# Seven down products in another order, splits between convolution steps and a rearranged last norm: a hybrid encoder block on one Trainium2 core

## The chip, the cores and the metric

The kernel runs on one core of one Trainium2 chip. The metric is the device time of one execution in microseconds (us). An execution has one TensorE (PE, matmuls; its weight loads are listed as PEld), VectorE (DVE), ScalarE (ACT), GpSimd (POOL) and a queue of transfers that SyncE issues (SP). Every engine works through its own list of instructions in order and waits where an operand, a buffer or a bank of PSUM is not ready. The kernel before took 1299.77 us (median of three runs, 1299.09 to 1300.25).

## The reference

A sequence of 1024 frames plus 16 meta tokens, 1024 wide, passes one layer: a mixer (retention heads and forgetting-attention heads), then a gated feed-forward part with a causal convolution, then a last RMS norm. All arithmetic is float32. The change touches the feed-forward part and the last norm only:

```
up = einsum('bld,df->blf', h, w_up)          # 1024 -> 2 x 2816
a, b = split(up, 2)
acc = conv_b + sum_j a_pad[:, j:j+L] * conv_w[j]     # 3 taps
h = h + einsum('blf,fd->bld', silu(acc) * b, w_down) # 2816 -> 1024
out = h * rsqrt(mean(h*h) + eps) * final_norm_g      # per frame
```

## The kernel before, in words

Everything is kept transposed: features lie on the 128 partitions, frames along the free axis. The result is eight tiles `H[0..7]` of 128 features x 1024 frames (`H0` is the first half of the frames, columns 0 to 511, `H1` the second).

**Up stage.** The 2816 hidden features are 22 tiles (`ft`). For each, the up projection is done as seven half-size products in place of eight (Strassen's scheme in Winograd's form, `SEQ`); then `conv1` and `conv2` do the convolution, SiLU and the gate, `u`, and `tsum` makes the differences T1 to T4 that the down stage needs of it. `u` and the T tiles are stored to HBM (`uB..`, `uT..`). `sd_sum` makes the sums S1 to S4 of the down weights and stores those (`wS..`).

**Down stage.** Again seven products of 512-wide halves (`DSEQ`): each is a sum over 11 k-tiles (`KH`), and each k-tile has a weight tile and an activation tile, loaded from HBM into `d_raw` and split into a high and a low fp32r part by `d_unit` (ACT casts the high part, `split_u`, L1197; DVE subtracts for the low part, L1198). A k-tile is then 4 blocks `j` x 3 matmuls (high x high, high x low, low x high), `d_mm`, L1384. With `g` counting k-tiles over all products, the main loop over `g` issues the matmuls of `g` and then splits ahead, up to k-tile `g + 4`. Split units live in a ring: six for the first six k-tiles (shared with the up stage), then twelve. Banks `X` (psa, psc) collect products 0, 2, 4, 6, banks `Y` (psb, psx) products 1, 3, 5; products 0, 1 and 4 start a fresh sum. `d_post` adds a finished sum to `H`.

The seven products run as 0, 1, 2, 3, 4, 5, 6. Product 0 reads the plain weights `A11` and `uB11`; product 1 reads `S2` and `T2`, whose last tile comes from the last `ft`. Product 5 finishes the lower four `H` tiles in `H0`, product 4 their `H1`, product 2 the upper four in `H0`, and product 6 the upper four in `H1`.

**Last norm.** Frames are taken in three chunks, `FCH`: chunk 0 is `H0` (512 frames), chunks 1 and 2 are the halves of `H1` (256 each). `sq_add` squares on ACT and adds on POOL (chunk 0) or DVE; `f_norm` sums over partitions with a matmul by ones (`nps`), takes the root, makes diagonal matrices (`dg`) and spreads the factor with a matmul (`pr`); `f_emit` multiplies, on ACT and POOL or on DVE by the bit masks `OUTE`, and SP stores. In product 6 the last three k-tiles (`NL = 3`) are held back and done as two halves of 256 frames, block by block, so that `H1` can be added, squared and summed block by block.

PE, DVE, ACT and POOL follow the written program order (`tc.manual_schedule`); the order of SP's transfers is chosen by the framework's scheduler.

Of the kernel before, what the change touches and what calls it, by code (L numbers as in the profile page):

```python
# [81 lines left out]
def tile_hymba_block(ctx, tc, xt, xn, wrv0, wrv1, wft, wout, wup, wdn, small, cst, rope, dtab, out):  # L82
# [1181 lines left out]

    cas, us = {}, {}

    def conv1(ft):
# [3 lines left out]
        act.activation(ca, at[:, 0:NF], AF.Copy, scale=cw[0])  # L1271
        dve.scalar_tensor_tensor(ca, at[:, 1:1 + NF], cw[1], ca, op0=ALU.mult, op1=ALU.add)
# [104 lines left out]
    X = Y = None  # L1377

    def d_mm(g, j, c, n, new):
        i, kt = divmod(g, KH)  # L1380
        a_, b_ = d_units[g, 0], d_units[g, 1]
        ps = (X, Y)[i in (1, 3, 5)][j]
        for m, (wi, hl) in enumerate(((0, 0), (0, 1), (1, 0))):
            pe.matmul(ps[:, c:c + n], lhsT=a_[:, wi, j * P:(j + 1) * P], rhs=b_[:, hl, c:c + n],  # L1384
                      start=(new and m == 0), stop=(kt == KH - 1 and m == 2), skip_group_check=i in (2, 3, 5, 6))
# [3 lines left out]
    with tc.manual_schedule(engines=ENG):  # L1389
# [256 lines left out]
        for g in range(6, 8):  # L1646
# [25 lines left out]
        def sq_add(ci, d):  # L1672
            c0, n = FCH[ci]
            hsl = H[d][:, c0:c0 + n]
            if ci not in acs:
                acs[ci] = es.tile([P, n], F32, name=f"ac{ci}")
                act.activation(acs[ci], hsl, AF.Square)
            else:
                sq = es.tile([P, 512], F32, tag="sq4", name="sq4", bufs=4)[:, :n]
                act.activation(sq, hsl, AF.Square)  # L1680
                (pool if ci == 0 else dve).tensor_tensor(acs[ci], acs[ci], sq, op=ALU.add)  # L1681

        prd = {}

        def f_norm(ci):
            c0, n = FCH[ci]
            m = n // P
            ps = (pb, px)[ci % 2].tile([P, 512], F32, tag=("psb", "psx")[ci % 2], name="nps")
            for j in range(m):
                pe.matmul(ps[:, j:j + 1], lhsT=acs[ci][:, j * P:(j + 1) * P], rhs=ones, start=True, stop=True)  # L1690
# [1 line left out]
            act.activation(r, ps[:, :m], AF.Sqrt, bias=epsc, scale=1.0 / 1024)
            dve.reciprocal(r, r)
            pr = (pb, px)[ci % 2].tile([P, 512], F32, tag=("psb", "psx")[ci % 2], name="pr")[:, :n]
            for j in range(m):
                dg = es.tile([P, P], F32, tag="dg", name="dg", bufs=4)
                dve.tensor_scalar(dg, idf, r[:, j:j + 1], None, op0=ALU.mult)  # L1697
                pe.matmul(pr[:, j * P:(j + 1) * P], lhsT=on, rhs=dg, start=True, stop=True)  # L1698
            prd[ci] = [pr, None]
            if OUTE[ci]:  # L1700
                prd[ci][1] = es.tile([P, n], F32, name=f"prs{ci}")
                act.copy(prd[ci][1], pr)

        fo = {}

        def f_emit(ci, d):
            c0, n = FCH[ci]
            pr, prs = prd[ci]
            m = 512 // n
            if d % m == 0:  # L1710
                fo[ci] = es.tile([P, m, n], F32, tag="fo", name="fo", bufs=8)
            ot = fo[ci][:, d % m, :]
            hsl = H[d][:, c0:c0 + n]
            g = sm[:, S_LG + d:S_LG + d + 1]
            if OUTE[ci] & (1 << d):
                act.activation(ot, hsl, AF.Copy, scale=g)  # L1716
                pool.tensor_tensor(ot, ot, prs, op=ALU.mult)
            else:
                dve.scalar_tensor_tensor(ot, hsl, g, pr, op0=ALU.mult, op1=ALU.mult)  # L1719
            if d % m == m - 1:  # L1720
                sp.dma_start(out[(d + 1 - m) * P:(d + 1) * P, c0:c0 + n].rearrange("(a p) n -> p a n", p=P), fo[ci])

        NL = 3
        for g in range(7 * KH):
            i, kt = divmod(g, KH)
# [14 lines left out]
            if i == 5 and 2 <= kt < 10:  # L1740
                if kt < 6:
                    sq_add(0, kt - 2)
                elif kt < 10:
                    sq_add(1, kt - 2)
                    sq_add(2, kt - 2)
            if i == 6:
                if kt in (1, 2):
                    sq_add(0, 2 + 2 * kt)
                    sq_add(0, 3 + 2 * kt)
                if kt == 3:  # L1750
                    f_norm(0)
                if 4 <= kt < 8:
                    f_emit(0, 2 * kt - 8)
                    f_emit(0, 2 * kt - 7)
            for _ in range(3):
                if d_next[0] < 2 * (g + 5):
                    d_unit()
        for hf in range(2):
            for j in range(4):
                for g in range(7 * KH - NL, 7 * KH):  # L1760
                    d_mm(g, j, 256 * hf, 256, False)
                hsl = H[j][:, 512 + 256 * hf:768 + 256 * hf]
                dve.tensor_tensor(hsl, X[j][:, 256 * hf:256 * hf + 256], hsl, op=ALU.add)  # L1763
# [84 lines left out]
```

## Time and profile before

| | |
|---|---|
| median of three runs | 1299.77 us |
| profiled execution: its own time, its span | 1297.7 us, 1295.6 us |
| PE / PEld busy, share of the span | 97% / 92% |
| DVE, ACT, POOL busy | 71%, 45%, 28% |
| transfers: mean busy share, whole span | 46.6% |
| down stage, first matmul to last output | from 1056.96 us to the end |

The profiled execution's span is 2.1 us under its own time. Times within it are given from the start of the span. The views used below: the table of busy time and granted clock in chosen stretches; the list of waits, which names for each engine whom it waited for; and the instructions in order of time, where one row may stand for several equal neighbours (x6) and the bracket gives the idle time ahead and what ended it. In the rows, L1384 is the matmul line of `d_mm`, L1197 and L1198 the two halves of a split, L1690 and L1698 the two small matmuls of the norm, L1763 the last addition into `H1`.

### The profile page before, as it was taken

The numbers are of one execution on the slowest core, as the hardware profiler recorded it, in microseconds if no ns is written. First come the engines' busy times: TensorE is split into PE (matmuls) and PEld (weight loads), VectorE is DVE, ScalarE is ACT, GpSimd is POOL, SyncE is SP. The second block draws the span as 40 slices with busy tenths as digits, with TensorE's granted clock in tenths as the row PEclk, the third lists the DMA queues.
The fourth block names the chain that finished last, engine by engine and source line by source line (L and its number), as shares of the span: only waits on it lengthen the run. The fifth ranks groups of instructions, "written<-read, shape, count | busy, mean of one in ns | idle before, by whom it ended". The sixth has DMA issues, their size and how long they took to land. (4 is left out here: it accounts for less than half of the span.)

```text
span 1295.6 us, 24143 instructions
## 1 busy us (share of the span) xinstructions
PE 1253.1 (97%) x9243; PEld 1187.8 (92%) x9243; DVE 916.6 (71%) x1571; ACT 589.4 (45%) x1171; POOL 365.2 (28%) x301
## 2 busy tenths in 40 slices
PE   8999999999999989989899999999999989999995
PEld 8999999999999989989899999999999988888884
DVE  5776546556565666658978778788898976855565
ACT  7773442456445553545533334334343335444552
POOL 0154244000000000022166456465464632300132
PEclk9999999999999999999999999999999999999998
DMA  8533124114223535364255354355655679666633
GB/s 284 178 95 97 36 68 128 38 44 124 52 62 95 156 109 166 102 206 131 69 193 163 118 167 143 127 180 176 222 183 184 212 263 348 233 195 192 190 104 117
DMA packets 110947, 192.76 MB, mean 149 GB/s; under 512 B 15143, under 2 KB 50295, under 8 KB 110832
## 3 DMA queue, kind: packets, MB, share of 16 engines
q1 hardware_dynamic: 110832, 191.23, 46.6%
q8 instruction: 72, 1.18, 0.4%
q14 instruction: 43, 0.35, 0.1%
HBM read 132.59 MB, written 52.21 MB: 143 GB/s over the span
## 5 line engine op out<-in xcount | busy, mean ns | idle before, releaser
L1198 DVE TENSOR_TENSOR d_u<-d_raw,d_u 128x512 fp32r<-128x512 f32 x154 | 118.0, 820 | 60.7 <-ACT d_u L1197 60.6
L1197 ACT CAST d_u<-d_raw 128x512 fp32r<-128x512 f32 x154 | 87.1, 619 | 95.1 <-PE psx L1384 44.3
L666 PE MATMUL psD<-xl,f_hi 128*128 128x256 f32 (+2 forms) x448 | 129.3, 289 | 0.0
L666 PE MATMUL psD<-xh,f_hi 128*128 128x256 f32 (+2 forms) x448 | 128.1, 286 | 0.4 <-DVE fq L672 0.4
L666 PE MATMUL psD<-xh,f_lo 128*128 128x256 f32 (+2 forms) x448 | 128.2, 286 | 0.0
L1193 POOL TENSOR_TENSOR S<-u_raw 128x512 f32<-128x512 f32 x42 | 59.0, 1406 | 202.9 <-DVE unit L1211 168.9
L1232 PE MATMUL psb<-B0T,unit 128*128 128x256 f32 x780 | 104.0, 282 | 1.0 <-DVE unit L1211 0.9
L1232 PE MATMUL psb<-B1T,unit 128*128 128x256 f32 x780 | 103.4, 281 | 0.7 <-ACT B1T L1158 0.6
L797 ACT ACTIVATE pf<-psS 128x272 f32<-128x272 f32 (+4 forms) x112 | 49.7, 451 | 114.0 <-PE psS L787 67.3
L1232 PEld LDWEIGHTS psb<-B0T,unit 128*128 128x128 f32 x780 | 97.2, 189 | 1.7 <-DVE unit L1211 1.4
L1232 PEld LDWEIGHTS psb<-B1T,unit 128*128 128x128 f32 x780 | 97.1, 189 | 1.1 <-ACT B1T L1158 0.8
L666 PEld LDWEIGHTS psD<-xh,f_hi 128*128 128x128 f32 x448 | 84.7, 189 | 0.9 <-DVE fq L672 0.6
L666 PEld LDWEIGHTS psD<-xl,f_hi 128*128 128x128 f32 x448 | 84.4, 188 | 0.4
L666 PEld LDWEIGHTS psD<-xh,f_lo 128*128 128x128 f32 x448 | 84.5, 189 | 0.1
L1390 POOL MEMSET on<- 128x128 f32 x1 | 0.2, 205 | 297.0 <-PE psS L791 297.0
L1211 DVE TENSOR_TENSOR unit<-S,unit 128x512 fp32r<-128x512 f32 x87 | 78.7, 906 | 2.6 <-ACT unit L1207 2.3
L733 DVE TENSOR_REDUCE mx<-psS 128x1 f32<-128x512 f32 (+6 forms) x120 | 59.0, 539 | 29.8 <-PE psS L730 20.9
L183 PE MATMUL psj<-rv_hi,xh 128*128 128x256 f32 (+1 forms) x264 | 76.3, 293 | 2.6 <-DVE z L287 2.2
L1207 ACT CAST unit<-S 128x512 fp32r<-128x512 f32 x87 | 54.1, 622 | 53.3 <-POOL S L1193 52.6
L1271 ACT ACTIVATE ca<-at,sm 128x1024 f32<-128x1024 f32 x22 | 25.3, 1152 | 112.5 <-DVE at L1263 112.5
L184 PE MATMUL psj<-rv_lo,xh 128*128 128x256 f32 (+1 forms) x264 | 75.5, 288 | 0.2 <-DVE rv_lo L118 0.2
L185 PE MATMUL psj<-rv_hi,xl 128*128 128x256 f32 (+1 forms) x264 | 75.3, 288 | 0.0
(347 smaller groups left out, 3581.8 us busy)
## 6 DMA issues: line engine op xcount, KB each, us to landing
u_raw<-wup SPq DMA_DIRECT2D x44, 512.0 KB
sd<-wdn SPq DMA_DIRECT2D x88, 128.0 KB
uB<-u SPq DMA_DIRECT2D x44, 256.0 KB
wS<-sd SPq DMA_DIRECT2D x88, 128.0 KB
d_raw<-wS SPq DMA_DIRECT2D x44, 256.0 KB
d_raw<-uT SPq DMA_DIRECT2D x44, 256.0 KB
d_raw<-wdn SPq DMA_DIRECT2D x33, 256.0 KB
d_raw<-uB SPq DMA_DIRECT2D x33, 256.0 KB
```

The lines of the kernel that those rows point to most:

```text
L183: pe.matmul(ps[:, :w], lhsT=x_h, rhs=w_h[:, c0:c0 + w], start=(k == 0), stop=False)
L184: pe.matmul(ps[:, :w], lhsT=x_h, rhs=w_l[:, c0:c0 + w], start=False, stop=False)
L185: pe.matmul(ps[:, :w], lhsT=x_l, rhs=w_h[:, c0:c0 + w], start=False, stop=(k == KT - 1))
L666: pe.matmul(ps[:, :n], lhsT=w_, rhs=X(e, k, t0 + a, n), start=(k == 0 and i == 0), stop=(k == KT - 1 and i == 2))
L733: dve.tensor_reduce(mxs[s][:R - q_, j, ci:ci + 1], ps[:R - q_, :n], axis=mybir.AxisListType.X, op=ALU.max)
L797: act.activation(pf[:r, a:b], ps[:r, a:b], AF.Exp)
L1193: (eng or pool).tensor_tensor(t, s_[x], s_[y], op=o)
L1197: act.copy(t[:, 0], src)
L1198: eng.tensor_tensor(t[:, 1], src, f(t[:, 0]), op=ALU.subtract)
L1207: act.copy(t[:, 0], srcs[ft][nm])
L1211: dve.tensor_tensor(t[:, 1], srcs[ft][SEQ[i][0]], f(t[:, 0]), op=ALU.subtract)
L1232: pe.matmul(ps[:, :n], lhsT=w[:, wi, k * P:(k + 1) * P], rhs=o[:, hl, k, :], start=(new and j == 0), stop=(j == 11), skip_group_check=not new)
```

## The change

- **Order of the products.** `DORD = (1, 0, 3, 2, 5, 4, 6)`: banks now alternate Y, X, Y, X, Y, X, X. Product 4 and product 6 are neighbours in the same banks, so each block's sum of product 4 is added to `H` (`d_post(4, j)`) ahead of that block's first matmul of product 6.
- **Splits in the last convolution.** Six more `d_unit` calls stand between the steps of the last `ft`: one ahead of `post(.., 6, 1)`, one inside `conv1`, two ahead of `conv2`, two behind it. Five k-tiles are thus split, or given out to be, before the down loop starts, where it was two.
- **Unit ring in two pools.** The ring of twelve is now eight buffers (`du`) and four (`du2`), used in the same turn.
- **Chunk 0 of the norm is earlier.** Products 5 and 2 are done after the fifth place, so squares are taken in places five and six, and `nps`, root, `dg` and `pr` of chunk 0 stand in the sixth place (its k-tiles 6, 8 and 9). Its eight outputs are emitted in the last product, one per k-tile, all on DVE.
- **Last product.** `NL` goes from 3 to 5. `f_norm` is cut in four (`f_nps`, `f_dg`, `f_bc`, `f_prs`) that stand apart, with matmuls of the next block between them. The last squares are not added on DVE but summed by more `nps` matmuls (`last`). `dg` is made on ACT but for one. The lower four outputs of chunk 1 and three of chunk 2 are pre-scaled on ACT (`f_pre`) and finished on POOL. The last two outputs of chunk 2 are stored one by one.

```
@@ the last ft @@
         d_unit()
         post(NFT - 1, 6, 0)
+        d_unit()
         post(NFT - 1, 6, 1)
-        conv1(NFT - 1)
+        conv1(NFT - 1, d_unit)
+        for _ in range(2):
+            d_unit()
         conv2(NFT - 1)
+        for _ in range(2):
+            d_unit()
         for _ in tsum(NFT - 1):
             pass
...
+    DORD = (1, 0, 3, 2, 5, 4, 6)
...
-            i, kt = divmod(g, KH)
+            i, kt = DORD[g // KH], g % KH
...
-        pl, nb = (Wu, 6) if g < 6 else (dp[1], 12)
+        lo = (d_next[0] - 13) % 12 < 8
+        pl, nb = (Wu, 6) if g < 6 else (dp[1], 8) if lo else (dp[2], 4)
...
-                (pool if ci == 0 else dve).tensor_tensor(acs[ci], acs[ci], sq, op=ALU.add)
+                if ci and d > (2, 2, 1)[ci] and d < 4:
+                    last[ci].append(sq)
+                else:
+                    (pool if ci == 0 and d < 4 else dve).tensor_tensor(acs[ci], acs[ci], sq, op=ALU.add)
...
+            src = [acs[ci]] + last.get(ci, [])
             for j in range(m):
-                pe.matmul(ps[:, j:j + 1], lhsT=acs[ci][:, j * P:(j + 1) * P], rhs=ones, start=True, stop=True)
+                for x, a_ in enumerate(src):
+                    pe.matmul(ps[:, j:j + 1], lhsT=a_[:, j * P:(j + 1) * P], rhs=ones,
+                              start=(x == 0), stop=(x == len(src) - 1))
...
-        NL = 3
+        NL = 5
         for g in range(7 * KH):
-            i, kt = divmod(g, KH)
-            if i < 6 or kt < KH - NL:
+            pos, kt = divmod(g, KH)
+            if pos < 6 or kt < KH - NL:
                 for j in range(4):
-                    d_mm(g, j, 0, 512, i in (0, 1, 4) and kt == 0)
-            if i and kt == 0:
+                    if pos == 6 and kt == 0:
+                        d_post(4, j)
+                    d_mm(g, j, 0, 512, DORD[pos] in (0, 1, 4) and kt == 0)
+            if 0 < pos < 6 and kt == 0:
                 for j in range(4):
-                    d_post(i - 1, j)
+                    d_post(DORD[pos - 1], j)
...
+            if pos == 5:
+                if 1 <= kt < 5:
+                    sq_add(0, 3 + kt)
+                if kt == 6:
+                    f_nps(0)
+                if kt == 8:
+                    f_dg(0)
+                if kt == 9:
+                    f_bc(0)
+            if pos == 6:
+                if kt < 4:
+                    sq_add(1, 4 + kt)
+                    sq_add(2, 4 + kt)
+                if kt < KT:
+                    f_emit(0, kt)
...
+                if hf and j == 0:
+                    f_nps(1)
+                    f_dg(1)
+                if hf and j == 1:
+                    f_bc(1)
+                    f_prs(1)
+                    for d in range(4, KT):
+                        f_emit(1, d, True)
                 sq_add(1 + hf, j)
-                if hf and j == 1:
-                    f_norm(1)
-        for d in range(KT):
+                if hf and j < 3:
+                    f_pre(2, 4 + j)
+        f_nps(2)
+        for d in range(3):
             f_emit(1, d)
-        f_norm(2)
-        for d in range(KT):
+        f_dg(2)
+        f_emit(1, 3)
+        f_bc(2)
+        f_prs(2)
+        for d in (4, 5, 6):
+            f_emit(2, d, True)
+        for d in (0, 1, 2, 3, 7):
             f_emit(2, d)
```

Three places show how instructions move. First DVE at the end of the last `ft` (`at`, `ca`, `u`, `T2o` are the last convolution's steps, `d_u` are low halves of splits), of before:

```order
L1263 TENSOR_TENSOR at<-psc,at 128x256 x2
L1272 SCALAR_TENSOR_TENSOR ca<-at,sm,ca 128x1024
L1273 SCALAR_TENSOR_TENSOR ca<-at,sm,ca 128x1024
L1288 TENSOR_TENSOR u<-bt,ca 128x1024
L1301 TENSOR_TENSOR T2o<-u,old 128x512
L1301 TENSOR_TENSOR T3o<-u,old 128x512
L1301 TENSOR_TENSOR T4o<-u,T2o 128x512
L1198 TENSOR_TENSOR d_u<-d_raw,d_u 128x512 x48
```

and of the change:

```order
L1198 TENSOR_TENSOR d_u<-d_raw,d_u 128x512
L1263 TENSOR_TENSOR at<-psc,at 128x256
L1272 SCALAR_TENSOR_TENSOR ca<-at,sm,ca 128x1024
L1198 TENSOR_TENSOR d_u<-d_raw,d_u 128x512
L1275 SCALAR_TENSOR_TENSOR ca<-at,sm,ca 128x1024
L1198 TENSOR_TENSOR d_u<-d_raw,d_u 128x512 x2
L1290 TENSOR_TENSOR u<-bt,ca 128x1024
L1198 TENSOR_TENSOR d_u<-d_raw,d_u 128x512 x2
L1303 TENSOR_TENSOR T2o<-u,old 128x512
L1303 TENSOR_TENSOR T3o<-u,old 128x512
L1303 TENSOR_TENSOR T4o<-u,T2o 128x512
L1198 TENSOR_TENSOR d_u<-d_raw,d_u 128x512 x20
```

Six low halves that stood behind all seven of these steps now stand among them.

Second, PE from the held-back k-tiles to the end (`nps` and `pr` are the norm's small matmuls), of before:

```order
L1384 MATMUL psa<-d_u 128x256 x18
L1384 MATMUL psc<-d_u 128x256 x18
L1384 MATMUL psa<-d_u 128x256 x18
L1690 MATMUL nps<-ones,ac_15198 128x1 x2
L1698 MATMUL pr<-dg,on_14203 128x128 x2
L1384 MATMUL psc<-d_u 128x256 x18
L1690 MATMUL nps<-ones,ac_15200 128x1 x2
L1698 MATMUL pr<-dg,on_14203 128x128 x2
```

and of the change, from the first block of the second half on:

```order
L1388 MATMUL psa<-d_u 128x256 x15
L1705 MATMUL nps<-ones,ac_15343 128x1
L1705 MATMUL nps<-ones,sq_15573 128x1
L1705 MATMUL nps<-ones,ac_15343 128x1
L1705 MATMUL nps<-ones,sq_15573 128x1
L1388 MATMUL psa<-d_u 128x256 x15
L1727 MATMUL pr<-dg,on_14441 128x128 x2
L1388 MATMUL psc<-d_u 128x256 x30
L1705 MATMUL nps<-ones,ac_15345 128x1
L1705 MATMUL nps<-ones,sq_15655 128x1
L1705 MATMUL nps<-ones,sq_15675 128x1
```

Fifteen matmuls of the next block now stand between chunk 1's `nps` and its `pr`.

Third, SP around the last `ft`'s stores in the change (`uT2_7604` is T2 in HBM; `d_raw` there is product 1's last k-tile):

```order
L1362 DMA d_raw_13841<-wS2_7608 128x512
L1362 DMA d_raw_13886<-wdn 128x512
L1362 DMA d_raw_13886<-uB11_7599 128x512
L1777 DMA H0_13844<-hs0_7584 128x1024
L1294 DMA uB21_7601<-u_13791 128x512
L1294 DMA uB22_7602<-u_13791 128x512
L1304 DMA uT2_7604<-T2o_13801 128x512
L1304 DMA uT3_7605<-T3o_13804 128x512
L1304 DMA uT4_7606<-T4o_13807 128x512
L1362 DMA d_raw_13841<-uT2_7604 128x512
L1362 DMA d_raw_13908<-wdn 128x512
```

The load of T2's last tile, which stood eleven k-tiles further on before, now follows the store that writes it by three places.

More of the change, by code (lines that the diff above doesn't have):

```diff
@@ L1272, in conv1 @@
         dve.scalar_tensor_tensor(ca, at[:, 1:1 + NF], cw[1], ca, op0=ALU.mult, op1=ALU.add)
+        if mid is not None:
+            mid()
         dve.scalar_tensor_tensor(ca, at[:, 2:2 + NF], cw[2], ca, op0=ALU.mult, op1=ALU.add)
@@ L1645, in tile_hymba_block @@
         dp[1] = mk(do, "du", side="right")
-        for g in range(6, 8):
+        dp[2] = mk(do, "du2", side="right")
+        for g in range(6, 6 + d_next[0] // 2):
             d_load(g)
@@ L1680, in sq_add, with f_nps @@
                 act.activation(sq, hsl, AF.Square)
-                (pool if ci == 0 else dve).tensor_tensor(acs[ci], acs[ci], sq, op=ALU.add)
-        prd = {}
-        def f_norm(ci):
+                if ci and d > (2, 2, 1)[ci] and d < 4:
+                    last[ci].append(sq)
+                else:
+                    (pool if ci == 0 and d < 4 else dve).tensor_tensor(acs[ci], acs[ci], sq, op=ALU.add)
+        dgd, prd, fo, last = {}, {}, {}, {1: [], 2: []}
+        def f_nps(ci):
             c0, n = FCH[ci]
@@ L1691, in f_norm, with f_dg @@
+        def f_dg(ci):
+            m = FCH[ci][1] // P
             r = es.tile([P, 4], F32, tag="fr", name="fr", bufs=3)[:, :m]
-            act.activation(r, ps[:, :m], AF.Sqrt, bias=epsc, scale=1.0 / 1024)
+            act.activation(r, prd[ci][:, :m], AF.Sqrt, bias=epsc, scale=1.0 / 1024)
             dve.reciprocal(r, r)
-            pr = (pb, px)[ci % 2].tile([P, 512], F32, tag=("psb", "psx")[ci % 2], name="pr")[:, :n]
+            dgd[ci] = []
             for j in range(m):
                 dg = es.tile([P, P], F32, tag="dg", name="dg", bufs=4)
-                dve.tensor_scalar(dg, idf, r[:, j:j + 1], None, op0=ALU.mult)
+                if ci == 2 and j == 0:
+                    dve.tensor_scalar(dg, idf, r[:, j:j + 1], None, op0=ALU.mult)
+                else:
+                    act.activation(dg, idf, AF.Copy, scale=r[:, j:j + 1])
+                dgd[ci].append(dg)
@@ L1698, in f_norm, with f_bc, f_prs @@
+        def f_bc(ci):
+            c0, n = FCH[ci]
+            pr = (pb, px)[ci % 2].tile([P, 512], F32, tag=("psb", "psx")[ci % 2], name="pr")[:, :n]
+            for j, dg in enumerate(dgd[ci]):
                 pe.matmul(pr[:, j * P:(j + 1) * P], lhsT=on, rhs=dg, start=True, stop=True)
             prd[ci] = [pr, None]
-            if OUTE[ci]:
+        def f_prs(ci):
+            c0, n = FCH[ci]
+            pr = prd[ci][0]
+            if ci:
                 prd[ci][1] = es.tile([P, n], F32, name=f"prs{ci}")
@@ L1702, in f_norm, with f_out, f_pre @@
                 act.copy(prd[ci][1], pr)
-        fo = {}
-        def f_emit(ci, d):
+        def f_out(ci, d):
+            m = 512 // FCH[ci][1]
+            if (ci, d - d % m) not in fo:
+                fo[ci, d - d % m] = [es.tile([P, m, FCH[ci][1]], F32, tag="fo", name="fo", bufs=8), 0]
+            return fo[ci, d - d % m]
+        def f_pre(ci, d):
             c0, n = FCH[ci]
-            pr, prs = prd[ci]
+            act.activation(f_out(ci, d)[0][:, d % 2, :], H[d][:, c0:c0 + n], AF.Copy, scale=sm[:, S_LG + d:S_LG + d + 1])
@@ L1709, in f_emit @@
+        def f_emit(ci, d, pre=False):
+            c0, n = FCH[ci]
             m = 512 // n
[L1710 to L1717, printed above, removed]
-            else:
-                dve.scalar_tensor_tensor(ot, hsl, g, pr, op0=ALU.mult, op1=ALU.mult)
@@ L1720, in f_emit @@
-            if d % m == m - 1:
-                sp.dma_start(out[(d + 1 - m) * P:(d + 1) * P, c0:c0 + n].rearrange("(a p) n -> p a n", p=P), fo[ci])
-        NL = 3
+            t = f_out(ci, d)
+            ot = t[0][:, d % m, :]
+            if pre:
+                pool.tensor_tensor(ot, ot, prd[ci][1], op=ALU.mult)
+            else:
+                dve.scalar_tensor_tensor(ot, H[d][:, c0:c0 + n], sm[:, S_LG + d:S_LG + d + 1], prd[ci][0],
+                                         op0=ALU.mult, op1=ALU.mult)
@@ L1724, in tile_hymba_block @@
+            t[1] += 1
+            if ci == 2 and d > 5:
+                sp.dma_start(out[d * P:(d + 1) * P, c0:c0 + n], ot)
+            elif t[1] == m:
+                d0 = d - d % m
+                sp.dma_start(out[d0 * P:(d0 + m) * P, c0:c0 + n].rearrange("(a p) n -> p a n", p=P), t[0])
+        NL = 5
         for g in range(7 * KH):
-            i, kt = divmod(g, KH)
-            if i < 6 or kt < KH - NL:
+            pos, kt = divmod(g, KH)
+            if pos < 6 or kt < KH - NL:
                 for j in range(4):
-                    d_mm(g, j, 0, 512, i in (0, 1, 4) and kt == 0)
@@ L1739, in tile_hymba_block @@
                 pool.memset(on, 1.0)
[L1740 to L1754, printed above, removed]
+            if pos == 4 and 2 <= kt < 6:
+                sq_add(0, kt - 2)
+            if pos == 5:
[13 more added lines that the diff above has]
+                    f_emit(0, kt)
             for _ in range(3):
@@ L1763, in tile_hymba_block @@
                 dve.tensor_tensor(hsl, X[j][:, 256 * hf:256 * hf + 256], hsl, op=ALU.add)
+                if hf and j == 0:
[4 more added lines that the diff above has]
+                    f_prs(1)
+                    for d in range(4, KT):
+                        f_emit(1, d, True)
                 sq_add(1 + hf, j)
-                if hf and j == 1:
-                    f_norm(1)
-        for d in range(KT):
+                if hf and j < 3:
+                    f_pre(2, 4 + j)
+        f_nps(2)
+        for d in range(3):
             f_emit(1, d)
-        f_norm(2)
-        for d in range(KT):
+        f_dg(2)
[5 more added lines that the diff above has]
+        for d in (0, 1, 2, 3, 7):
             f_emit(2, d)
```

11 lines of the change are left out of this document (7 added, 4 removed).

## The prediction

> **What bounds the kernel now.** PE is busy 97% of the span, so only its gaps and its clock are to be had. I first read its waits from 1036 us to the end:
>
> ```profile
> PE pr L1698 <- DVE dg L1697: 5.8, 3, 2.6
> PE psa L1384 <- DVE d_u L1198: 3.9, 2, 2.9
> PE nps L1690 <- DVE ac L1681: 1.6, 1, 1.6
> PE psa L1384 <- ACT d_u L1197: 1.1, 1, 1.1
> ```
>
> That is 12.4 us: splits that come late (d_u) and the norm's small matmuls (pr, nps). Then the stretches, with PE's busy time first, and behind POOL's the granted clock, the share of the DMA engines and GB/s:
>
> ```profile
> 1057.00:1067.10 10.10, 6.11 (x27) 4.47 (x25) 7.37 (x10) 5.41 (x8) 0.00 (x0) 1.00 1.00 347
> 1067.10:1071.40 4.30, 4.29 (x12) 3.40 (x13) 2.36 (x4) 0.00 (x0) 0.00 (x0) 0.60 1.03 378
> 1071.40:1253.30 181.90, 181.90 (x804) 150.60 (x803) 115.83 (x162) 87.43 (x157) 29.38 (x20) 1.00 0.65 217
> 1253.30:1257.40 4.10, 3.21 (x24) 2.87 (x23) 1.05 (x5) 1.03 (x3) 0.00 (x0) 1.00 0.00 0
> 1278.70:1282.40 3.70, 3.63 (x21) 3.33 (x19) 0.89 (x3) 0.79 (x2) 0.00 (x0) 0.60 0.00 0
> 1282.40:1295.60 13.20, 1.77 (x8) 1.45 (x8) 6.55 (x18) 2.25 (x6) 2.13 (x3) 0.63 0.46 160
> ```
>
> For 182 us in the middle PE has no gap at full clock: the order of the products by itself is worth nothing there. What can be won lies at the start of the down stage, in its last product, and in the 13.2 us behind the last block. Twice a gap is followed by a clock of 0.60.
>
> **The start.** These rows, in order of time, tell how the first k-tiles run dry:
>
> ```profile
> 1056.96 1.55 PE L1384 MATMUL psa<-d_u 128*128 128x512 f32 x6
> 1058.87 1.29 DVE L1272 SCALAR_TENSOR_TENSOR ca<-at,sm,ca 128x1024 f32<-128x1024 f32 x1 [1.28 <-ACT ca L1271]
> 1062.56 3.20 ACT L1197 CAST d_u<-d_raw 128x512 fp32r<-128x512 f32 x6
> 1062.69 1.23 DVE L1288 TENSOR_TENSOR u<-bt,ca 128x1024 f32<-128x1024 f32 x1 [1.22 <-ACT ca L1286]
> 1063.74 0.51 PE L1384 MATMUL psa<-d_u 128*128 128x512 f32 x1 [1.14 <-ACT d_u L1197]
> 1063.95 0.69 DVE L1301 TENSOR_TENSOR T2o<-u,old 128x512 f32<-128x512 f32 x1
> 1065.77 3.69 DVE L1198 TENSOR_TENSOR d_u<-d_raw,d_u 128x512 fp32r<-128x512 f32 x6
> 1067.11 1.93 PE L1384 MATMUL psa<-d_u 128*128 128x512 f32 x5 [2.87 <-DVE d_u L1198]
> 1074.24 1.36 PE psa L1384 x6
> 1227.26 1.29 DVE L1198 TENSOR_TENSOR d_u<-d_raw,d_u 128x512 fp32r<-128x512 f32 x2 [1.42 <-ACT d_u L1197]
> ```
>
> Six matmuls take 1.36 us, so a k-tile of twelve takes 2.72 us, and PE wants k-tile g at 1056.96 + 2.72 g. Two k-tiles were split ahead; the third's casts stand on ACT behind the SiLU, its subtractions on DVE behind u and T2 to T4. So PE waits 1.14 + 2.87 = 4.01 us, and the 4.30 us at a clock of 0.60 lose 4.30 x 0.40 = 1.72 us more.
>
> In the change six subtractions of 0.65 us (1.29 for two) stand among these steps. I walk DVE forward from its first convolution step: that ends at 1060.16, one split 1060.81 (k-tile 2, wanted at 1062.40), second step 1062.1, two splits 1063.4 (k-tile 3, wanted 1065.12), u 1064.6, two splits 1065.9 (k-tile 4, wanted 1067.84), T2 to T4 1068.0, k-tile 5 at 1069.3 (wanted 1070.56). The margins are 1.3 to 1.9 us; ACT's casts, 0.53 us each in its row of six, fit into its waits for DVE. Raw k-tiles must have landed by then; those up to 5 are issued ahead of the down stage in both orders. I take the whole 5.73 us. The bounds: nothing, if another wait takes its place (a rival below), to all.
>
> The price is T2: u ends 1.9 us later than before, T2 at about 1066.6 in place of 1064.64, and its last tile is now wanted as k-tile 10, at 1056.96 + 27.2 = 1084.2, by way of HBM.
>
> ```profile
> 1069.31 0.95 SPq L1292 DMA_DIRECT2D uB<-u  x2
> 1070.66 0.32 SPq L1302 DMA_DIRECT2D uT<-T2o  x1
> 1076.54 7.39 ACT L1197 CAST d_u<-d_raw 128x512 fp32r<-128x512 f32 x14 [3.88 <-DMA uB<-u]
> ```
>
> Before, T2 was ready at 1064.64 and its store was issued only at 1070.66, behind loads, with the DMA engines full (share 1.00). The store of u landed at 1076.5, 7.2 us after the first issue. With one H load and one k-tile load fewer ahead of it in SP's order I put T2's store at 1069.5, landed 6.5 us later, its load as long again, split 1.3 us after that: 1083.8, 0.4 us early. The backlog drains meanwhile, since SP has little else to issue, so I expect some 2 us of slack and charge nothing. The other stores hide as before. The two-pool ring makes only k-tiles 10 and 11 wait for the old u and T buffers, where before k-tile 6 did (the 3.88 us of ACT above).
>
> [...]
>
> **The last product.**
>
> ```profile
> 1242.24 1.37 DVE L1667 TENSOR_TENSOR H<-psx,H 128x512 f32<-128x512 f32 x2
> 1228.46 0.75 DVE L1681 TENSOR_TENSOR ac<-ac,sq 128x256 f32<-128x256 f32 x2
> 1255.43 1.16 PE L1698 MATMUL pr<-dg,on 128*128 128x128 f32 x8 [0.89 <-DVE dg L1697]
> 1258.95 11.49 POOL L1717 TENSOR_TENSOR fo<-fo,prs 128x512 f32<-128x512 f32 x7 [10.11 <-ACT fo L1716]
> 1260.03 9.26 DVE L1198 TENSOR_TENSOR d_u<-d_raw,d_u 128x512 fp32r<-128x512 f32 x6 [0.97 <-ACT d_u L1197]
> 1269.21 0.73 DVE L1719 SCALAR_TENSOR_TENSOR fo<-H,sm,pr 128x512 f32<-128x512 f32 x1
> 1269.35 1.58 PE L1384 MATMUL psa<-d_u 128*128 128x256 f32 x11 [1.01 <-DVE d_u L1198]
> 1270.65 2.23 PEld L1384 LDWEIGHTS psc<-d_u 128*128 128x128 f32 x18
> 1272.81 2.23 PEld L1384 LDWEIGHTS psa<-d_u 128*128 128x128 f32 x18
> 1278.25 0.71 PE L1698 MATMUL pr<-dg,on 128*128 128x128 f32 x4 [2.40 <-DVE dg L1697]
> ```
>
> Gone: 0.89 us (chunk 0's root, now two k-tiles, 5.4 us, ahead of its pr); 1.01 us (splits that took 9.26 / 6 = 1.54 us beside POOL's products); 2.40 us (chunk 1's pr, which now has fifteen matmuls ahead of it, 1.8 us against a root and dg of about 1.3); and the clock of 0.60 for 3.70 us, 1.48 us. Together 5.78 us.
>
> Whether 1.01 us goes hangs on DVE, which takes over POOL's outputs. From the last k-tile of product 4 to the last split it has four additions of 0.685, seven outputs of 0.71, six sums of 0.375 and fourteen splits of 0.645: 19.0 us. It starts when product 4's first block is done, 2.0 us ahead of the last product, so it ends about 17.0 us into it. PE comes to that unit after six k-tiles (16.3) and twelve half matmuls at 2.16 / 18 = 0.12 us: 17.8. Spare: 0.8 us. d_post(4, j) itself is 0.7 us against the 2.04 us that three other blocks take. I charge nothing; the other bound is 1 us late plus a slow clock.
>
> Added on PE: 24 matmuls of 512 become 48 of 256, 48 x 0.12 - 24 x 0.227 = 0.32 us, and two more nps matmuls, about 0.6 us. Up to the last block the gain is 5.73 + 5.78 - 0.92 = 10.6 us.
>
> **Behind the last block.**
>
> ```profile
> 1282.88 0.42 ACT L1680 ACTIVATE sq<-H 128x256 f32<-128x256 f32 x1 [1.50 <-DVE H L1763]
> 1283.90 0.58 PE L1690 MATMUL nps<-ones,ac 128*128 128x1 f32 x4 [1.57 <-DVE ac L1681]
> 1284.52 0.26 ACT L1692 ACTIVATE fr<-nps,epsc 128x2 f32<-128x2 f32 x1 [0.82 <-PE nps L1690]
> 1286.42 0.16 DVE L1693 RECIPROCAL fr<-fr 128x2 f32<-128x2 f32 x1
> 1286.61 0.48 DVE L1697 TENSOR_SCALAR dg<-idf,fr 128x128 f32<-128x128 f32 x2
> 1288.73 2.44 DVE L1719 SCALAR_TENSOR_TENSOR fo<-H,sm,pr 128x256 f32<-128x256 f32 x6 [1.64 <-issue]
> 1289.13 1.41 POOL L1717 TENSOR_TENSOR fo<-fo,prs 128x256 f32<-128x256 f32 x2 [4.63 <-ACT fo L1716]
> ```
>
> On the old clock: the square ends at 1283.30; nps starts at 1283.44 with eight of its twelve matmul records behind it (0.58 / 4 each): 1284.60, no better than 1284.48. Then the root, 1284.90; the reciprocal at once, since only three outputs of 0.41 stand ahead on DVE (before it waited 1.64 us for seven): 1285.1; dg, one on DVE and one on ACT. An ACT operation of 128x128 is in no row; between 0.26 (128x2) and 0.42 (128x256) I take 0.35: 1285.5. pr 0.71: 1286.3. The five outputs on DVE start 0.5 us after pr, as before, and end at 1288.8; POOL's three of 0.70, behind the copy of pr, at 1288.9. Before, the last output ended at 1291.17 and the span 4.43 us later; so 2.3 us are won. Bounds: 1 us (the stores set the end) to 3 us (a full clock under nps and pr).
>
> **The sum.** 10.6 + 2.3 = 12.9 us off a span of 1295.6: 1282.7. The profiled execution took 1297.7, 2.1 above its span and 2.07 under the median, so on the scale of the median 1299.77 - 12.9 = 1286.9; I write 1287. Its own range is 1284 to 1290.
>
> **The rivals.** (1) *T2's round trip is late.* For: 0.4 us of margin at the full queue's latency. Against: the queue drains. With both legs a little slower PE stands 2 us at k-tile 10 and loses 1.7 us of clock: 1290.6. Chance 0.15. (2) *DVE becomes the bound in the last product.* For: 0.8 us spare in 19. Against: POOL, beside which a split took 1.54 us, is idle there. A tenth slower is 1.1 us late, with the clock 2.6: 1289.5. Chance 0.09. (3) *The slow clock stays though the gaps go*: its two stretches then still cost 1.72 + 1.48 = 3.2 us: 1290.1. Against: both begin at a gap's end. [...] Chance 0.06. (4) *The gains are hidden*: the full DMA queue, not the order of splits, feeds PE at the start; DVE eats what the last product's waits leave; the stores set the tail. Then 1 us in the tail stands against 0.92 us added on PE: 1299.7, no change within 0.2%, which is 2.6 us and about what a measurement of this kernel can tell. Against: the DMA share falls to 0.65 right after, and what ACT waited for was the store of u, not a raw k-tile. Chance 0.03. (5) *Slower.* One mechanism: SP works in order, so everything behind T2's load (k-tile 12's load, the H loads) waits for its store, which waits for u, which waits for splits, which wait for PE's buffers: one loop around the queue. It decides once T2's load lands after 1084.2 - 1.3 = 1082.9; each us later costs one; 12.9 + 2.6 us later, at 1098.4, the kernel is slower than before by what can be told: 1302.5. Against: the store would have to land three times as late as the 7.2 us seen. Chance 0.03.
>
> **How the numbers follow.** The forecast has 0.64, the rivals 0.15, 0.09, 0.06, 0.03, 0.03. Rivals 1 to 3 are faster too: 0.94 faster, 0.03 the same, 0.03 slower. The range starts at 1284 (the tail's 3 us, and margins as computed with a little more in the norm) and ends at 1293, which takes in rivals 1 to 3 and two of them together.
>
> **What would show it.** Right: no wait of PE for d_u between 1057 and 1085; a clock of 1.00 from there to the last block; product 6 without a wait for d_u; chunk 1's pr with no gap; about 11 us from the last block to the end, where it was 13.3. Wrong: a gap of PE at k-tile 10 named by ACT or DVE behind a load of uT; a gap at the first held-back k-tiles; a slow clock with no gap ahead of it; a last block later than 1273 us.

## The result

The changed kernel took 1283.47 us (median; 1282.62 to 1289.05), the kernel before 1299.66 us beside it (1299.09 to 1300.25): a ratio of 0.9884, 95% interval 0.9856 to 0.9913. Measured again (e1) the two stood at 1286.78 and 1301.38 us, 0.9893 (0.9857 to 0.9928). The forecast was 1287 us and a gain of 12.9; the gains are 16.2 and 14.6 us, and the first median lies 0.5 us under the low end of the range.

The profiled execution of the changed kernel is the slowest of its first four: 1289.05 us, span 1287.2. Its PE waits from 1036 us to the end are these (in all, times, longest), where before there were four rows and 12.4 us:

```profile
PE pr L1727 <- DVE dg L1718: 1.0, 1, 1.0
PE nps L1705 <- ACT sq L1690: 0.7, 1, 0.7
```

Both stand behind the last block. The stretches, with PE busy first and the granted clock behind POOL's column, as they were shown of before (the last product begins at 1243.41 us, within the third row):

```profile
1057.00:1067.10 10.10, 10.10 (x67) 9.21 (x66) 7.14 (x11) 3.57 (x6) 0.26 (x1) 1.00 0.97 332
1067.10:1071.40 4.30, 4.30 (x21) 3.56 (x20) 4.28 (x7) 3.15 (x5) 0.00 (x0) 1.00 1.05 383
1071.40:1253.30 181.90, 181.90 (x812) 150.88 (x811) 119.74 (x176) 90.98 (x165) 23.20 (x16) 1.00 0.68 231
1253.30:1257.40 4.10, 4.10 (x20) 3.40 (x19) 4.10 (x7) 1.33 (x3) 0.00 (x0) 1.00 0.39 152
1257.40:1273.00 15.60, 15.60 (x123) 15.17 (x123) 7.18 (x17) 6.84 (x18) 0.49 (x1) 1.00 0.12 45
1273.00:1287.20 14.20, 5.20 (x38) 4.76 (x37) 5.43 (x14) 2.42 (x7) 4.61 (x7) 0.67 0.43 148
```

PE has no gap and a clock of 1.00 from the start of the down stage to the end of the last block at 1275.62 us. The start and T2's trip through HBM, in order of time:

```profile
1061.99 1.55 PE L1388 MATMUL psb<-d_u 128*128 128x512 f32 x6
1068.49 1.23 DVE L1290 TENSOR_TENSOR u<-bt,ca 128x1024 f32<-128x1024 f32 x1
1072.91 0.32 SPq L1304 DMA_DIRECT2D uT<-T2o  x1
1078.91 0.32 SPq L1362 DMA_DIRECT2D d_raw<-uT  x1
1082.14 2.71 ACT L1197 CAST d_u<-d_raw 128x512 fp32r<-128x512 f32 x5 [3.11 <-DMA d_raw<-uT]
```

The first down matmul comes at 1061.99 us, 5.03 us later than in the profile of before (1056.96), though PE's instructions ahead of it are the same, and those of ACT and DVE too up to the first added split, whose cast on ACT starts 2.6 us ahead of it. Compared matmul by matmul, the changed kernel's profile is already 4.1 us late at 213 us of the span, and so is that of e12, which is the kernel before, unchanged. So I read each profile in three parts: up to the first down matmul, from there to the end of the last block (the matmuls of d_mm), and the rest of the span.

| profile | first down matmul | to the last block's end | rest | from the first down matmul |
|---|---|---|---|---|
| before | 1056.96 | 225.37 | 13.27 | 238.64 |
| before, again (e12) | 1061.23 | 225.96 | 13.31 | 239.27 |
| changed | 1061.99 | 213.63 | 11.58 | 225.21 |
| changed, again (e1) | 1058.72 | 213.63 | 11.05 | 224.68 |
| e2 splits only | 1058.11 | 223.81 | 14.08 | 237.89 |
| e3 order only | 1057.83 | 225.91 | 13.56 | 239.47 |
| e4 one ring | 1061.11 | 217.39 | 11.40 | 228.79 |
| e5 no early splits | 1056.24 | 219.77 | 11.39 | 231.16 |
| e6 outputs on POOL | 1058.92 | 217.36 | 11.42 | 228.78 |
| e7 three held back | 1056.54 | 214.10 | 11.16 | 225.26 |

From the first down matmul on, the gain is 13.4 us between the two first profiles, 14.6 between the two repeats. Two profiles of one kernel differ there by 0.5 to 0.6 us, and ahead of it by 3.3 to 4.3 us. Up to the last block's end the changed kernel repeats to 0.01 us: e9 to e11, which differ from it only behind that point, have 213.62 there.

### The profile page after: what moved, and what is told of

It is laid out like the page before. It is cut to its first block, busy times and chain, and to the rows that moved or that the text cites. A ratio compares the mean times of both kernels' runs of the same rounds, so it can differ in the third digit from the quotient of the medians.

```text
span 1287.2 us, 24215 instructions
## 1 busy us (share of the span) xinstructions
PE 1253.1 (97%) x9279; PEld 1189.2 (92%) x9279; DVE 910.1 (71%) x1568; ACT 588.8 (46%) x1174; POOL 348.7 (27%) x294
## 4 chain that ended last, share of the span: by engine, by line
PE 82%; DVE 6%; issue 4%; DMA 3%; ACT 3%; POOL 1%; SPq 0%; POOLq 0%; DVEq 0%; ACTq 0%
PE psb L1232 13%; PE psD L666 12%; PE psc L1232 9%; PE psa L1232 9%; PE psO L824 4%; PE psD L894 4%; PE psb L1388 3%; PE psx L1388 3%; PE psa L1388 3%; PE psc L1388 3%; PE psS L787 3%; PE psj L183 2%; PE psj L185 2%; PE psj L184 2%; PE psS L730 2%
## 5 line engine op out<-in xcount | busy, mean ns | idle before, releaser
L1198 DVE TENSOR_TENSOR d_u<-d_raw,d_u 128x512 fp32r<-128x512 f32 x154 | 110.0, 760 | 53.6 <-ACT d_u L1197 53.4
```

The source lines that it names most:

```text
L1198: eng.tensor_tensor(t[:, 1], src, f(t[:, 0]), op=ALU.subtract)
```

## Experiments

**e1 and e12: each kernel again.**

> The changed kernel again, unchanged, to tell the down stage from what lies ahead of it. My terms: from the first matmul of the down stage to the end 225.2 us again (before: 238.6), so a gain of 13.4 us whatever the profiled execution's own time; the instructions ahead of it are the same in both kernels, so the first down matmul should come at 1056 to 1062 us in both, by chance. If that holds, the median gains 13 to 14 us, near 1286. Rival: the change also shortens what lies ahead of the down stage; then the first down matmul comes at 1056 or earlier and the median stays at 1283.5, 16 us under before.

> The kernel before, unchanged, for a second reading of its parts: if the parts are steady, 238.6 us from the first down matmul to the end within 1 us, with the first down matmul anywhere between 1056 and 1062 us. Rival: the down stage itself varies by several us, and the comparison of single profiles by parts does not hold.

Measured: see the table. Both down stages repeat within 0.6 us and both first down matmuls move by chance: over all profiles of this study they lie between 1056.24 (e5) and 1069.35 us (e10), with the same instructions of PE ahead. In the profile of e12 the clock in the stretch from 180 to 240 us was 0.94, in that of before 1.00; that far the difference can be placed, its cause was not looked for. What follows: the 13.4 to 14.6 us are the change's, and what a median shows beside them is largely that chance. The rival, that the change shortens what lies ahead, has nothing for it: the changed kernel's two profiles have their first down matmul at 1061.99 and 1058.72, the two of before at 1056.96 and 1061.23.

**e2: the early splits alone, in the kernel before.**

```
         post(NFT - 1, 6, 0)
+        d_unit()
         post(NFT - 1, 6, 1)
-        conv1(NFT - 1)
+        conv1(NFT - 1, d_unit)
...
-        for g in range(6, 8):
+        for g in range(6, 6 + d_next[0] // 2):
```

> The kernel before with the six early splits alone: old order, one ring of twelve, old last product. Theory of the forecast: the stall of 4.0 us and the slow clock of 1.7 us go, 1294. Rival, from the 3.88 us that ACT waited for the store of u ahead of k-tile 6's cast: in one ring k-tile 6 lies in the memory of u and T, PE now comes to it at 16.3 us behind the first down matmul, and its cast cannot start before the store has landed some 19.6 us behind it; PE stands about 4.5 us there and loses 1.7 us of clock, so that the time stays at 1299 to 1300.

Measured: 1298.71 us, ratio 0.9972 (0.9950 to 0.9995); from the first down matmul 237.89 us, 0.75 us less than in before, and up to the last block 223.81, 1.6 us less. The two waits at k-tile 2 are gone, and a new one stands at k-tile 6. ACT first, then PE:

```profile
1075.72 7.39 ACT L1197 CAST d_u<-d_raw 128x512 fp32r<-128x512 f32 x14 [8.03 <-DMA uT<-T3o]
1076.91 3.31 PE L1386 MATMUL psa<-d_u 128*128 128x512 f32 x6 [2.29 <-ACT d_u L1197]
1080.02 1.65 PE L1386 MATMUL psc<-d_u 128*128 128x512 f32 x6
```

ACT waits 8.03 us for the stores of u and T to leave the memory that the ring takes. PE loses 2.29 us and then, with six matmuls taking 3.11 us to the next row's start where 1.36 is usual, 1.75 us of clock. The rival was right in kind, its wait of 4.5 us about twice the 2.29 measured: the stores were done by 17.6 us behind the first down matmul, where it had 19.6.

**e4: the changed kernel with one ring of twelve.**

```
-        pl, nb = (Wu, 6) if g < 6 else (dp[1], 8) if lo else (dp[2], 4)
+        pl, nb = (Wu, 6) if g < 6 else (dp[1], 12)
```

> The changed kernel with its ring of twelve units in one pool again, nothing else. Theory: the two pools keep k-tile 6 out of the memory of u and T; in one pool its cast waits for those stores, PE stands 3 to 5 us at k-tile 6 and the clock falls for some 4 us, 5 to 7 us lost against the changed kernel. Rival: the pools only fit the ring into memory and cost or bring nothing: within 1 us of the changed kernel.

Measured: 1290.84 us against 1286.78 of the changed kernel; 3.6 to 4.1 us more from the first down matmul. The same wait, in its own order of products:

```profile
1077.73 7.55 ACT L1197 CAST d_u<-d_raw 128x512 fp32r<-128x512 f32 x14 [7.04 <-DMA uB<-u]
1078.92 0.49 PE L1388 MATMUL psb<-d_u 128*128 128x512 f32 x1 [1.29 <-ACT d_u L1197]
1079.73 2.23 PE L1388 MATMUL psb<-d_u 128*128 128x512 f32 x5 [0.31 <-DVE d_u L1198]
1081.75 2.35 PE L1388 MATMUL psx<-d_u 128*128 128x512 f32 x6
1083.94 1.54 PE L1388 MATMUL psb<-d_u 128*128 128x512 f32 x6
```

1.6 us of wait and about 1.7 us of clock (the eleven matmuls from 1079.73 on take 4.21 us to the next row's start, where 2.49 is usual). The loss is under the 5 to 7 us expected and well over the rival's 1 us. So early splits and two pools are one step: the first brings PE to k-tile 6 before the old ring's memory is free, the second frees it.

**e5: the changed kernel without the early splits** (the six added `d_unit` calls taken out, `conv1` without its argument).

> The changed kernel with the splits back behind the last convolution; order, two pools, norm and last product as changed. Theory: the 4.0 us stall at k-tile 2 and the slow clock behind it come back, and the two pools still spare k-tile 6: 5.7 us more from the first down matmul to the end, about 230.7 us in place of 225. Rival (the splits matter little, the pools do most): under 3 us more.

Measured: 231.16 us from the first down matmul, 6.0 and 6.5 us more than the changed kernel's two profiles (median 1290.74). Both old waits are back to a tenth:

```profile
PE psb L1388 <- DVE d_u L1198: 2.9, 1, 2.9
PE psb L1388 <- ACT d_u L1197: 1.1, 1, 1.1
```

**e3: the order alone, in the kernel before** (`DORD` in `d_load` and `d_mm`, `d_post` by it, squares moved to where their sums are ready).

> The kernel before with the new order of the seven products alone (and the squares moved to where their sums are ready: chunk 0 in the sixth place, chunks 1 and 2 in the last product). Theory: the order by itself is worth nothing, PE keeps its 4.0 us stall at the start, a gap at chunk 0's and chunk 1's pr, and the held-back k-tiles: 1299 to 1301, since DVE gets 2.3 us of sums more in the last product. Rival: the order itself brings a part, 3 us or more.

Measured: 1300.28 us, ratio 0.9992 (0.9966 to 1.0017); 239.47 us from the first down matmul. All waits of before are there, those of the start now at banks Y:

```profile
PE pr L1699 <- DVE dg L1698: 5.9, 3, 2.6
PE psb L1385 <- DVE d_u L1198: 2.9, 1, 2.9
PE nps L1691 <- DVE ac L1682: 1.6, 1, 1.6
PE psb L1385 <- ACT d_u L1197: 1.1, 1, 1.1
PE psa L1385 <- DVE d_u L1198: 1.0, 1, 1.0
```

The order by itself is worth nothing: up to the last block 225.91 us, where before has 225.37 and 225.96. That it makes chunk 0's early norm possible is plain from the sums it needs; the early norm under the old order cannot be had, so this part was not tried apart.

**e6: seven outputs of chunk 0 on ACT and POOL again.**

```
                 if kt == 9:
                     f_bc(0)
+                    f_prs(0)
...
-                if kt < KT:
-                    f_emit(0, kt)
+                if kt < KT - 1:
+                    f_pre(0, kt)
+                    f_emit(0, kt, True)
+                elif kt < KT:
+                    f_emit(0, kt)
```

> The changed kernel with seven of chunk 0's eight outputs on ACT and POOL in the last product, as before, in place of DVE. Theory: a split takes up to 1.5 us on DVE beside POOL's products in place of 0.65, DVE comes to the last held-back unit 1 us or more after PE, and PE waits there 1 to 4 us with a slow clock behind it if the wait is over 2 us: 226 to 231 us from the first down matmul. Rival: taking 0.73 us of output per k-tile off DVE pays for the slower splits, no wait: 225 us.

Measured: 1289.80 us; 228.78 us from the first down matmul, 3.6 to 4.1 more. DVE's and then PE's rows in the last product:

```profile
1247.65 2.39 DVE L1198 TENSOR_TENSOR d_u<-d_raw,d_u 128x512 fp32r<-128x512 f32 x2
1250.63 3.49 DVE L1198 TENSOR_TENSOR d_u<-d_raw,d_u 128x512 fp32r<-128x512 f32 x2
1254.04 2.94 DVE L1694 TENSOR_TENSOR ac<-ac,sq 128x256 f32<-128x256 f32 x2
1242.09 1.65 PE L1388 MATMUL psa<-d_u 128*128 128x512 f32 x6 [1.59 <-DVE H L1677]
1260.65 0.62 PE L1388 MATMUL psa<-d_u 128*128 128x256 f32 x3 [0.58 <-DVE d_u L1198]
1261.86 0.38 PE L1388 MATMUL psa<-d_u 128*128 128x256 f32 x1 [0.58 <-DVE d_u L1198]
```

While POOL works, splits take up to 1.2 and 1.75 us and a sum of 128x256 up to 1.47 (means of the rows), where in the changed kernel they take 0.64 and 0.38. PE waits twice 0.58 us at the held-back units, as expected. The 1.59 us at the seam between products 4 and 6 are the experiment's own: `f_prs(0)` puts a copy on ACT that waits for PE's pr, the casts behind it come late, DVE's splits with them (6.73 us of wait for ACT), and DVE's addition of product 4 stands behind those. So it is shown that DVE is slower while POOL works (in before, too, a split took 1.54 us beside POOL's products), and 1.2 us of wait follow at the held-back units; how much of those goes back to the late casts at the seam was not tried apart.

**e7: three k-tiles held back in place of five** (`NL = 3`).

> The changed kernel with three k-tiles held back in place of five. Theory: nine matmuls of 0.12 us (1.1 us) between chunk 1's nps and pr do not cover root and dg (1.8 us in the trace of the changed kernel), PE stands 0.7 us there, and the chain of addition, square and sum of 1.3 us per block falls behind PE's 1.1 us per block, so that the last block's chain is 0.5 to 1 us later; 0.3 us of matmul time is saved: 0.5 to 2 us more from the first down matmul to the end. Rival: nothing hangs on five, within 0.3 us, or 0.3 us less.

Measured: 1285.93 us; 225.26 us from the first down matmul, 0.05 and 0.6 more than the changed kernel's two. PE's waits there, and the one that lies ahead of the last block:

```profile
PE nps L1705 <- ACT sq L1690: 1.0, 3, 0.5
PE pr L1727 <- DVE dg L1718: 1.0, 1, 1.0
1265.89 0.38 PE L1705 MATMUL nps<-ones,sq 128*128 128x1 f32 x2 [0.46 <-ACT sq L1690]
```

Up to the last block it has 214.10 us, 0.47 more than the 213.62 to 213.63 of the changed kernel, the low end of the expectation and over the rival's 0.3. The place is another than expected: PE does not wait for chunk 1's dg (its pr has no gap) but 0.46 us for its square, ahead of nps. So five are worth about 0.5 us, by one profile; the medians do not tell the two apart.

**e8: gaps of four lengths made on PE.**

```
+            ng = {(4, 3): 1, (4, 7): 2, (5, 2): 3, (5, 7): 5}.get((pos, kt))
...
+                act.copy(gp[:, 0:1], Z[1][:, 0:1])
+                for _ in range(ng):
+                    act.activation(gp, gp, AF.Copy)
+                pe.matmul(Z[0][:, 0:1], lhsT=gp[:, :P], rhs=ones, start=True, stop=True)
```

> The changed kernel with four gaps made on PE, in the fifth and sixth products: PE waits for a chain of one, two, three and five ACT copies of 128x512 (about 1.0, 1.6, 2.2 and 3.5 us with what starts the chain). It adds work and leaves none out. By the traces before (0.9 and 1.0 us gaps without a slow clock, 2.4 and 2.9 us with one) the clock should fall behind the two longer ones, 3 to 4 us at 0.6 each, and stay at 1.00 behind the shorter two. [...]

The waiting matmul with its gap in brackets, and the rows of six behind it, for each of the four:

```profile
1193.75 0.38 PE L1794 MATMUL psa<-ones,gp 128*128 128x1 f32 x2 [0.97 <-ACT gp L1793]
1193.99 1.64 PE L1388 MATMUL psb<-d_u 128*128 128x512 f32 x6
...
1206.89 0.38 PE L1794 MATMUL psa<-ones,gp 128*128 128x1 f32 x2 [1.63 <-ACT gp L1793]
1207.13 1.63 PE L1388 MATMUL psb<-d_u 128*128 128x512 f32 x6
...
1226.13 0.38 PE L1794 MATMUL psx<-ones,gp 128*128 128x1 f32 x2 [2.29 <-ACT gp L1793]
1226.38 2.91 PE L1388 MATMUL psa<-d_u 128*128 128x512 f32 x6
1229.08 1.89 PE L1388 MATMUL psc<-d_u 128*128 128x512 f32 x6
...
1246.53 0.38 PE L1794 MATMUL psx<-ones,gp 128*128 128x1 f32 x2 [3.61 <-ACT gp L1793]
1246.77 2.82 PE L1388 MATMUL psa<-d_u 128*128 128x512 f32 x6
```

Behind gaps of 0.97 and 1.63 us six matmuls take the usual time; behind 2.29 and 3.61 us they take 2.6 to 2.7 us from start to start where 1.36 is usual. A gap of 2.29 us is enough, as expected. By its rows, about 1.7 us are lost besides the gap (2.70 and 1.73 us for six where 1.36 is usual).

These gaps alone give no threshold: in e4 eleven matmuls were 1.7 us slower behind waits of 1.29 and 0.31 us, 1.60 together, where 1.63 us left the usual time here. The clock records tell more; I read those of the first profiles of before and of the changed kernel. In both, every time between two changes of the granted clock is a whole multiple of 3.41 us. Ahead of the last block's end each stretch at 0.50 is 3.41 us long, as from 1067.80 to 1071.21 and from 1279.42 to 1282.84 us in before, which costs a busy PE 1.7 us; behind it the clock is 0.50 to the end of the span, from 1286.25 us in before and from 1277.75 in the changed kernel. I cut the time behind 1056 us into lengths of 3.41 us that begin and end where these changes lie, and took for each the time that PE spent without a matmul wider than one column (the others taken at 0.227 us for 512 columns, 0.12 for 256 and 0.09 for 128, from the rows). Of the 129 lengths at full clock the four with 2.30 us or more of such time are followed by one at 0.50, and none of the 125 with 1.84 us or less is: in before 2.83 (from 1064.38 us), 2.49 (1276.01) and 3.41 (1282.84), in the changed kernel 2.30 (1274.33). By that reading it would count how much of one length is idle, so where a gap lies and not its size alone; that this is what parts the 1.63 us here from the waits of e4 is the author's estimate from these two profiles, and no run was made to test it.

**e9 to e11: the end behind the last block.** e9 turns the two loops of `f_nps` (sources outside, blocks inside); e10 adds ten matmuls that keep PE busy in the two gaps; e11 also issues the last store from ACT's queue. In all three the second block's first matmul, with `start`, now stands ahead of the first block's last one in the same tile `ps`, and the output is not the reference's (relative error 0.75). That this order is the reason was not tried apart. Their times are read for the end alone, where instructions and waits are in place.

```
-            for j in range(m):
-                for x, a_ in enumerate(src):
+            for x, a_ in enumerate(src):
+                for j in range(m):
...
+                if ci == 2 and x:
+                    f_warm((4, 6)[x - 1])
...
-                sp.dma_start(out[d * P:(d + 1) * P, c0:c0 + n], ot)
+                (act if d == 7 else sp).dma_start(out[d * P:(d + 1) * P, c0:c0 + n], ot)
```

> The changed kernel with the loops of f_nps turned (sources outside, blocks inside), so that in the last chunk only two of six small matmuls, four of twelve records, stand behind the last square. Theory: eight records cost 1.1 us behind the square, four about 0.5: 0.5 us less behind the last block, 11.05 to 11.6 us before, 10.5 to 11.1 now, if the clock is the same. Rival: DVE, which has three outputs and one addition there, sets the root's successor, and nothing is won.

> The same with ten matmuls of 128x256 that compute nothing used, four in the gap of 0.7 us ahead of the last nps and six in the gap of 1.0 us ahead of the last pr. Theory: the clock fell to 0.5 in this stretch because PE is idle or has one-column matmuls; kept busy it stays at 1.00 and pr takes 0.6 to 0.7 us, never 1.2. Rival: the clock is set by the gaps behind pr, the extra matmuls only delay pr by 0.1 to 0.3 us.

> The same, and the last output's store issued from ACT's queue in place of SP's, where it stood 0.5 us behind another. Theory: the store lands 0.4 to 0.5 us sooner, 10 to 10.6 us from the last block to the end; from the first down matmul about 224 us (changed kernel 224.7 and 225.2); medians cannot tell this from the changed kernel, since executions of one kernel differ by several us ahead of the down stage. Rival: the store of the output before it ends last anyway, no gain over the kernel with the extra matmuls.

Measured from the last block's end to the end of the span: e9 11.15 us, e10 10.73, e11 10.81. PE's rows of the end in e10, with pr of the changed kernel's second profile (e1) behind them:

```profile
1283.17 0.58 PE L1710 MATMUL nps<-ones,sq 128*128 128x1 f32 x4
1284.18 0.50 PE L1710 MATMUL nps<-ones,sq 128*128 128x1 f32 x4
1285.65 0.68 PE L1734 MATMUL pr<-dg,on 128*128 128x128 f32 x4
...
1275.39 0.68 PE L1727 MATMUL pr<-dg,on 128*128 128x128 f32 x4 [0.97 <-DVE dg L1718]
```

From the last block's end to pr's start the changed kernel takes 3.03 us, and e1, e4, e5, e6 and e8, whose instructions there are the same, 3.04; e9 takes 2.59, e10 2.68, e11 2.67. So 0.45 us are saved in e9 and 0.36 in the other two, near the 0.5 expected. To the end of the span those six take 10.86 to 11.58 us, so the saving there is no larger than what varies between them.

pr took 1.19 us in the changed kernel's first profile and 0.68 in its second. In the first the clock was 0.50 from 1277.75 us on, ahead of pr (1278.65). In before the last pr took 1.19 us as well (at 1287.04, clock 0.50 from 1286.25 on), chunk 1's 0.71 at a clock of 1.00 (at 1278.25). pr took 1.19 us in e9, and 0.68 in e10 and e11, which have the extra matmuls. But 0.68 is also what e1's took without them, so that they shorten pr is not shown. The store on ACT's queue brought nothing: e11 is no shorter than e10, by one profile each. The medians (e11: 1286.26 us) cannot tell this from the changed kernel. No form of e9 with the right sums was run, so no version better than the changed kernel is shown.

## Why the prediction was right, and where it was off

**What bounds it.** Right: the middle gave nothing, and the order alone nothing (e3).

**The start.** Forecast 5.73 us; taking the splits out again costs 6.1 us up to the last block (e5: 219.77 against 213.63). The walk along DVE held: the waits at k-tiles 2 to 5 are gone. But the prediction priced the two pools only as k-tiles 10 and 11 waiting in place of k-tile 6, and charged nothing. They carry 3.8 us (e4: 217.39 against 213.63): without them the early splits win 1.6 us of their 5.73 (e2). The row was there, ACT's 3.88 us behind the store of u; in before PE was late enough not to feel it. The forecast's 5.73 stood because the pools are part of the change; what it left unsaid is that most of it hangs on them. One reading was off without effect: by its own walk u ends 0.7 us later than before and only T2 1.9; measured, from the first down matmul, 0.8 and 1.8.

**T2's round trip** (rival 1) did not bite, and was mis-sized in the careful direction. On the scale of the first down matmul T2's store was issued at +10.9 us, its load at +16.9, the cast began at +20.2; wanted at +27.2. So the store's landing took up to 6.0 us, close to the 6.5 taken, but the load 3.2, half of the 6.5 taken from the full queue. The slower rival, the loop around SP's queue, needs it to land at +41.4, 21 us later than it did.

**The slow clock** (rival 3) did not stay: both slow stretches went with their gaps, as the sum had it, and the clock is 1.00 from the start of the down stage to the end of the last block. In e8, behind a made gap of 2.29 us, six matmuls took 2.70 us where 1.36 is usual.

**The last product.** Forecast 5.78 - 0.92 = 4.86 us. Measured: 225.37 - 213.63 = 11.74 us in all, less the 6.1 of the start, 5.6. The mis-sized term is chiefly the 0.6 us for more nps matmuls. Rows of the changed kernel, first pr of chunk 0 and the first half's blocks, then chunk 1:

```profile
1239.79 1.05 PE L1727 MATMUL pr<-dg,on 128*128 128x128 f32 x8
1258.06 1.28 DVE L1198 TENSOR_TENSOR d_u<-d_raw,d_u 128x512 fp32r<-128x512 f32 x2
1259.73 3.75 PE L1388 MATMUL psa<-d_u 128*128 128x256 f32 x30
1269.31 0.36 PE L1705 MATMUL nps<-ones,sq 128*128 128x1 f32 x2
1269.53 2.04 PE L1388 MATMUL psa<-d_u 128*128 128x256 f32 x15
1271.41 0.61 PE L1727 MATMUL pr<-dg,on 128*128 128x128 f32 x4
1271.78 3.84 PE L1388 MATMUL psc<-d_u 128*128 128x256 f32 x30
```

pr holds the blocks up by 0.37 us, from its start to theirs, and chunk 1's nps, from 1268.72, by 0.81; before, nps and pr took from 1275.25 to 1278.72, 3.47 us with 2.40 of waiting. Without the waiting that is 1.07 us before and 1.18 now, 0.1 more and not 0.6, so this place gave 2.3 us where 2.40 - 0.6 = 1.8 was charged. Chunk 0's nps and pr took 2.75 us in before (1253.60 to 1256.35) and now 0.81 and 0.80, 1.14 us less where 0.89 was charged. The two differences, 0.5 and 0.25, lead from 4.86 to 5.6. DVE (rival 2) kept up: its last split ends at 1259.34, PE comes to it twelve half matmuls behind 1259.73, at about 1261.2, 1.8 us later, where 0.8 was computed.

**Behind the last block.** Forecast 2.3 us, measured 1.7 and 2.3. The term that was off is pr, taken at 0.71 us:

```profile
1276.64 0.38 PE L1705 MATMUL nps<-ones,sq 128*128 128x1 f32 x2 [0.69 <-ACT sq L1690]
1278.65 1.19 PE L1727 MATMUL pr<-dg,on 128*128 128x128 f32 x4 [0.96 <-DVE dg L1718]
```

That eight nps records behind the square eat what the left-out sum saves was right; e9 shows that 0.45 us of it lie in the order of those records.

**The sum.** 12.9 us forecast, 13.4 measured in the profiles that it was made for. That they lie so close is in part luck: up to the last block 11.7 us came where 10.6 were forecast, behind it 1.7 where 2.3 were. The further 2.8 us of the first median, and the place just under the range, are not explained by any step: the part ahead of the down stage, which the change does not touch, moves by more than that from one execution to the next.

## What to carry to other kernels

Work moved ahead of a stall brings the consumer to the next thing that it needs: ask which buffer that is and whose transfer still holds it, and cost that before the gain is written down. Where a kernel's executions differ by several us, compare profiles from a marker behind the part that varies; here that showed differences of 0.5 us (e7), which medians of several runs did not. And count a gap on PE like the 2.29 us of e2 and of e8 twice: each cost the gap and some 1.7 us of slower matmuls behind it.

## What was not expected of the hardware

The stretch ahead of the down stage, with the same instructions of PE, took between 1056.24 and 1069.35 us in the profiles of this study. Most of the delay against the first profile of before came early: the vst addition that stands there at 264.64 us came at 268.75 in the changed kernel, 268.73 in e12 and 274.89 in e10, 4.1, 4.1 and 10.3 us late, where the first down matmul was 5.0, 4.3 and 12.4 us late. And the clock did not go by the gaps of PE alone: in the changed kernel's first profile it fell to 0.50 at 1277.75 us with only 0.74 us of gaps in the 3.41 us ahead, but 2.30 us without a matmul wider than one column, while in e6 six matmuls behind a gap of 1.59 us took 1.65 us, about as long as those behind the gaps of 0.97 and 1.63 us in e8.
